# Staging buffers, splits and start blocks in a one-layer hybrid encoder: low weight blocks loaded into ystage, q and k split four blocks later, the first stick head two blocks later

## The chip, the cores and the metric

The kernel runs on one core of a Trainium2 chip. Its time is the device time of one execution in microseconds (us); the figure given for a kernel is the median of its runs. Five engines take part: PE (TensorE) multiplies, DVE (VectorE) and ACT (ScalarE) convert, scale and add, POOL (GpSimd) masks and issues the DMAs that add into their target, and SP (SyncE) issues the plain DMAs. Each engine takes its instructions in a fixed order, and a waiting instruction holds up all that stand behind it on its engine.

## The reference

One layer over 512 tokens of width 2048, all in float32:

```python
h = rms_norm(x, g0); P = h @ w_in                      # 11 blocks of 512 columns
y = concat(stick_breaking(q, k, v),                    # 8 heads of 64, causal
           differential(q, k, v, rel_bias),            # 4 heads, q and k 2 x 64
           rg_lru(...), short_conv(...))
x = x + rms_norm(y @ w_out, g1)
u = causal_dwconv(rms_norm(x, g2) @ w_up)              # 2048 x 8192
x = x + rms_norm((gelu(u[:, :4096]) * u[:, 4096:]) @ w_down, g3)
```

## The kernel before

Products are done in pairs of a rounded high part and a remainder ("hi" and "lo"), because PE multiplies in a rounded float32 form: an operand is cast by ACT (the hi part) and DVE subtracts to get the lo part. A weight chunk of 512 KB is loaded by SP into a `w_raw` tile, cast into `w_hi` and subtracted into `w_lo`; there are three buffers of each.

PE's order is written by hand. `group` (L127 to L180) walks eight chunks of a weight block over four output units; after every few matmuls it calls `tick()`, which advances a block counter, `clock[0]`, and runs the functions that `at(block, fn)` has put down for that block. A block of a plain group holds eight or four matmuls of 512 columns (8, 8, 4 and 4 in a chunk). So attention's small matmuls lie between the weight matmuls at fixed places, and the block numbers decide where.

The order of the other engines is not written by hand. A scheduler takes the program's instructions by a priority, which is their order in the program unless a `high_priority` block puts them ahead, and gives each engine what is ready in its own forecast of the run; what it has fixed is then each engine's order on the chip.

First half, groups 0 to 10 over `w_in`: 0 and 1 feed the recurrent branch, 2 is v of the stick heads, 3 and 4 their q and k, 5 is v of the differential heads, 6 and 7 their q and k, 8 to 10 the short convolution. `norm0` (L299) multiplies the sum of squares, `ssum`, by ones to get the first norm's factor; it stands at block 27, and group 0 ends with block 32. Lines 353 to 393 work out small parameters of the recurrent and the differential branch from the table `par`. `Scores.query` and `Scores.key` (L493, L504) evict a unit of q or k from PSUM by DVE, and return a function that splits it into hi and lo parts by ACT casts and DVE subtractions; `group` calls it right after the eviction. `stick` (L539) puts a head down from block t0: logits at t0 to t0+2, the sums at t0+7 to t0+9, weights at t0+9, values at t0+16; heads follow each other every 12 blocks, and the first starts two blocks after group 3 ends.

Second half: `w_out`, the residual and norm, then the FFN. Its first up columns are four plain groups: `up_plain(half, ts)` for both column halves over tokens 0 to 255 (H0), and then over tokens 256 to 511 (H1). All other up columns are 28 units (`up_unit`, numbers 4 to 31) of a Strassen-like scheme with seven products, `seven` (L1063): from the four blocks of a weight tile, a11, a12, a21 and a22, it forms s1 = a21 + a22, s2 = a11 + s1, s3 = a11 + a21 and s4 = a12 + s2, and multiplies in the order a11, a12, s2 ("T2"), s1 ("T1"), s3 ("T3"), s4 ("22"), a22 ("T4"). `raw` loads a block (SP), `dma_add` adds one into its target by a DMA from POOL (L1058), `add` adds by DVE (L1054), `operand` makes hi and lo (L1048, L1049), and `take` evicts a product (L1142 to L1145). Unit 4 is the first: its tiles a11, a12 and a21 are w_raw buffers, s3 and a22 are `spare[0]` and `spare[2]`, which lie in a "mg" buffer of the pool `wide` that is free only after `split_t2` has read it. The later units take a11 and a21 from `spare` and a12, s3 and a22 from w_raw.

The down part has four plain groups and then eight units (`down_unit`) through the same `seven`. Its operands are built by `build` (L1189 and on) from the gated values, which come in pairs through two staging pools, `ystage` and `gst`, of two buffers each; down unit 0 takes s3 from `ystage` and a22 from `gst`. In the up part nothing uses `ystage`.

Of the kernel before, what the change touches and what calls it, by code (L numbers as in the profile page):

```python
# [48 lines left out]
def trunk(ctx: ExitStack, tc: tile.TileContext, xT, params, consts, wgate, w_in, w_out, w_up0, w_up, w_dn, w_dns, out):  # L49
# [187 lines left out]
    with ExitStack() as ph:  # L237
# [83 lines left out]

        at(27, norm0)
        at(50, norm0_columns)
# [12 lines left out]
        def lru_group(pair, before=None):  # L336
            xs, gs = {}, {}

            def evac(u, ps):
# [5 lines left out]
                else:  # L345
# [7 lines left out]
        negb = ph1.tile([P, 8], F32, name="negb")  # L353
        V.tensor_scalar(out=negb, in0=par[:, PC["b_gate"]:PC["b_gate"] + 8], scalar1=-1.0, scalar2=0.0,
                        op0=ALU.mult, op1=ALU.add)
        lam_ap = par[:, PC["lam"]:PC["lam"] + 4]

        sp8 = ph1.tile([P, 4], F32, name="sp8")
# [4 lines left out]
        la_m = ph1.tile([P, 4], F32, name="la_m")  # L363
        V.scalar_tensor_tensor(out=la_e, in0=lam_ap, scalar=-1.0, in1=lam_ap, op0=ALU.mult, op1=ALU.max)
        A.activation(out=la_e, in_=la_e, func=AF.Exp, scale=-1.0)
        V.tensor_scalar(out=la_s, in0=la_e, scalar1=2.0, scalar2=0.0, op0=ALU.add, op1=ALU.add)
        V.reciprocal(out=la_s, in_=la_s)
        V.tensor_tensor(out=la_s, in0=la_s, in1=la_e, op=ALU.mult)
        V.tensor_tensor(out=la_q, in0=la_s, in1=la_s, op=ALU.mult)
        V.memset(la_m, 1.0 / 17)  # L370
        for n in (15, 13, 11, 9, 7, 5, 3, 1):
            V.tensor_tensor(out=la_m, in0=la_m, in1=la_q, op=ALU.mult)
            V.tensor_scalar(out=la_m, in0=la_m, scalar1=1.0 / n, scalar2=0.0, op0=ALU.add, op1=ALU.add)
        V.tensor_tensor(out=la_m, in0=la_m, in1=la_s, op=ALU.mult)
        V.tensor_scalar(out=la_e, in0=lam_ap, scalar1=-1.0, scalar2=0.0, op0=ALU.mult, op1=ALU.max)
        V.scalar_tensor_tensor(out=sp8, in0=la_m, scalar=2.0, in1=la_e, op0=ALU.mult, op1=ALU.add)
        V.tensor_scalar(out=sp8, in0=sp8, scalar1=8.0, scalar2=0.0, op0=ALU.mult, op1=ALU.add)
        V.tensor_scalar(out=nsp8, in0=sp8, scalar1=-1.0, scalar2=0.0, op0=ALU.mult, op1=ALU.add)

        lm = ph1.tile([P, 2], F32, name="lm")  # L380
        lmp = ph1.tile([P, 128], F32, name="lmp")
        dl = PC["dl"]
        for i in range(2):
            V.tensor_tensor(out=lmp[:, i * 64:(i + 1) * 64], in0=par[:, dl + 128 * i:dl + 128 * i + 64],
                            in1=par[:, dl + 128 * i + 64:dl + 128 * i + 128], op=ALU.mult)
            V.reduce_sum(out=lm[:, i:i + 1], in_=lmp[:, i * 64:(i + 1) * 64], axis=mybir.AxisListType.X)
        A.activation(out=lm, in_=lm, func=AF.Exp)
        lam = ph1.tile([P, 1], F32, name="lam")
        V.scalar_tensor_tensor(out=lam, in0=lm[:, 0:1], scalar=LAM_INIT, in1=lm[:, 1:2],
                               op0=ALU.add, op1=ALU.subtract)  # L390
        gsub = ph1.tile([P, 1], F32, name="gsub")
        V.tensor_scalar(out=gsub, in0=pc("sub_g"), scalar1=1.0 - LAM_INIT, scalar2=0.0,
                        op0=ALU.mult, op1=ALU.add)

# [92 lines left out]
        class Scores:  # L487
# [5 lines left out]
            def query(self, ps):  # L493
                f = t2()
                V.scalar_tensor_tensor(out=f, in0=ps, scalar=0.125, in1=rstd0, op0=ALU.mult, op1=ALU.mult)
                return lambda: self.split_query(f)

# [6 lines left out]
            def key(self, ps):  # L504
                f = t2()
                mul_rstd(f, ps)
                return lambda: self.split_key(f)

# [19 lines left out]
        def qk_group(g, dst):  # L528
            def evac(u, ps):
                return (dst[u // 2].query if u % 2 == 0 else dst[u // 2].key)(ps)  # L530
            in_group(g, evac)
# [6 lines left out]

        def stick(t0, pr, e, qk, vs):  # L539

# [101 lines left out]
        for g, prs in ((3, (0, 1)), (4, (2, 3))):  # L642
            qk = (Scores(), Scores())
            qk_group(g, qk)
            t0 = max(t0, clock[0] + 2)
            for i, pr in enumerate(prs):
                for e in range(2):
                    stick(t0, pr, e, qk[i], vs)
                    t0 += 12
# [134 lines left out]
    with ExitStack() as ph:  # L784
# [238 lines left out]
        ubs = up_ph.enter_context(tc.tile_pool(name="ubs", bufs=4))  # L1023
        for half in range(2):
            up_plain(half, H1)


        split_t2()
        ubp = ubs
        spare_t = wide.tile([P, 4, 4, S // 2], F32, name="mg")  # L1030
        spare = [spare_t[:, i] for i in range(4)]
        turn = [0]

# [6 lines left out]
        def raw(t, src):  # L1040
            with tc.high_priority(offset=AHEAD):
                w_load.append(nc.sync.dma_start(out=t, in_=by4(src)))
# [19 lines left out]

        def seven(src, tops, take, first=False, place=None):  # L1063

# [22 lines left out]
            if place is None:  # L1087
                a11, a21 = raw(spare[n], src[0, 0]), raw(spare[2 + n], src[1, 0])
                a12, s3, a22 = (w_raw() for _ in range(3))
            else:  # L1090
                a11, a12, a21 = (w_raw() for _ in range(3))
                s3, a22 = place
                raw(a11, src[0, 0])
                raw(a12, src[0, 1])
                raw(a21, src[1, 0])
            if first:
                raw(a22, src[1, 1])
                add(a21, a21, a22)
# [36 lines left out]
        def up_unit(unit):  # L1135
# [105 lines left out]
        def down_unit(n):  # L1241
            def take(i, ts, ps, first):
                u = 2 * n + i
                t = m3[u // 4][:, u % 4, ts]
                with tc.high_priority(offset=AHEAD):
                    for part in (ps[:, 0:256], ps[:, 256:512]):
                        V.tensor_tensor(out=t, in0=t, in1=part, op=ALU.subtract if i else ALU.add)  # L1247
# [173 lines left out]
```

## Time and profile before

| what | us |
|---|---|
| median of three runs (1768.4, 1771.96, 1774.53) | 1771.96 |
| the profiled execution | 1772.23 |
| its span, first to last instruction | 1770.5 |
| PE busy in the span | 1727.5 |
| DVE busy | 1252.2 |
| ACT busy | 902.1 |
| POOL busy | 162.0 |

The profiled execution lies 0.27 us over the median. 1.73 us of it lie outside the span. The page of the profile gives busy times, a chain of waits that ended last, and groups of instructions; the views of the trace give each engine's instructions in order of time with the idle time before them and what ended it, the waits in total, and busy time and granted clock by window.

### The profile page before, as it was taken

The page shows a single profiled execution, that of the slowest core. Times are in us where ns is not written, and L with a number is a line of the kernel's source. Part 1 is how long each engine was busy: PE and PEld are TensorE (multiplying, and loading weights), DVE is VectorE, ACT ScalarE, POOL GpSimd, SP SyncE. Part 2 cuts the span into 40 slices and gives each one's busy share as a digit, 9 for nine tenths or more (in the row PEclk, how much of TensorE's full clock was granted, in tenths as well). Part 3 has the DMA queues.
Part 4 walks back from the last instruction along what each step waited for, and adds up shares of the span by engine and source line. Part 5 has one row for each costly group of instructions (what it writes and reads, how often), then busy time and mean ns, then how long its engine had stood idle before and what let it go on. Part 6 is the DMA issues. An engine that isn't in the chain of part 4 may idle for free.

```text
span 1770.5 us, 24333 instructions
## 1 busy us (share of the span) xinstructions
PE 1727.5 (98%) x9152; PEld 1484.7 (84%) x9152; DVE 1252.2 (71%) x1926; ACT 902.1 (51%) x1351; POOL 162.0 (9%) x229
## 2 busy tenths in 40 slices
PE   8999999999999999999899999999999999999995
PEld 7778788887888888899888888888888888888884
DVE  7885565576656424799888888888878887775337
ACT  6443576665334235777555555555554673334342
POOL 0000011100000011100111111111111001100110
PEclk9999999999999999999999999999999999999998
DMA  7234222242223625775788898898888768878233
GB/s 258 80 102 144 74 79 87 78 154 73 93 86 101 208 96 173 236 225 184 220 237 252 231 231 217 229 239 230 223 238 225 211 203 229 215 198 280 96 116 134
DMA packets 97310, 309.14 MB, mean 175 GB/s; under 512 B 10500, under 2 KB 14852, under 8 KB 97192
## 3 DMA queue, kind: packets, MB, share of 16 engines
q1 hardware_dynamic: 80200, 247.81, 41.9%
q0 software_dynamic: 15840, 57.68, 17.5%
q10 hardware_dynamic: 1152, 2.10, 0.3%
q8 instruction: 72, 1.18, 0.3%
q14 instruction: 46, 0.38, 0.1%
HBM read 266.64 MB, written 21.24 MB: 163 GB/s over the span
## 4 chain that ended last, share of the span: by engine, by line
PE 89%; DVE 5%; DMA 3%; ACT 2%; issue 1%; POOLq 0%; POOL 0%; SPq 0%; DVEq 0%; ACTq 0%
PE mm L157 33%; PE mm L1079 24%; PE mm L1084 12%; PE pa L157 4%; PE pa L149 3%; PE mm L149 2%; PE mm L121 2%; PE mm L123 2%; PE mm L122 2%; PE pa L587 1%; DVE w_lo L100 1%; DMA w_raw<-in_w_up_dram 1%; DVE w_lo L1049 1%; PE pa L692 1%; DVE m L1298 0%
## 5 line engine op out<-in xcount | busy, mean ns | idle before, releaser
L100 DVE TENSOR_TENSOR w_lo<-w_raw,w_hi 128x1024 fp32r<-128x1024 f32 (+1 forms) x207 | 253.6, 1226 | 251.2 <-PE mm L157 141.1
L99 ACT CAST w_hi<-w_raw 128x1024 fp32r<-128x1024 f32 (+1 forms) x207 | 216.2, 1045 | 292.1 <-PE mm L157 195.1
L157 PE MATMUL mm<-a,w_hi 128*128 128x512 f32 (+1 forms) x1504 | 339.9, 377 | 2.1 <-DVE t L330 2.1
L157 PEld LDWEIGHTS mm<-a,w_hi 128*128 128x128 f32 x1504 | 267.1, 189 | 52.2 <-DVE t L330 2.6
L1079 PE MATMUL mm<-a,w_hi 128*128 128x512 f32 x1088 | 274.6, 395 | 6.8 <-DVE ub L1145 5.0
L1048 ACT CAST w_hi<-w_raw 128x1024 fp32r<-128x1024 f32 x146 | 153.1, 1050 | 201.7 <-PE mm L1079 169.0
L1079 PEld LDWEIGHTS mm<-a,w_hi 128*128 128x128 f32 x1088 | 197.0, 190 | 42.4 <-DVE ub L1145 5.4
L1049 DVE TENSOR_TENSOR w_lo<-w_raw,w_hi 128x1024 fp32r<-128x1024 f32 x146 | 178.4, 1222 | 39.0 <-ACT w_hi L1048 34.4
L157 PE MATMUL mm<-a,w_lo 128*128 128x512 f32 (+1 forms) x752 | 182.1, 380 | 0.0
L1084 PEld LDWEIGHTS mm<-a,w_lo 128*128 128x128 f32 x1088 | 148.9, 191 | 10.7
L157 PEld LDWEIGHTS mm<-a,w_lo 128*128 128x128 f32 x752 | 132.5, 190 | 24.0 <-issue 1.5
L1084 PE MATMUL mm<-a,w_lo 128*128 128x256 f32 x1088 | 152.1, 283 | 0.0
L1079 PE MATMUL mm<-xs,w_hi 128*128 128x512 f32 x576 | 144.5, 393 | 1.0 <-DVE ub L1145 1.0
L1048 ACT CAST w_hi<-mg 128x1024 fp32r<-128x1024 f32 x83 | 86.6, 1044 | 86.9 <-PE mm L1079 84.9
L1079 PEld LDWEIGHTS mm<-xs,w_hi 128*128 128x128 f32 x576 | 103.8, 189 | 19.9 <-DVE ub L1145 1.4
L1049 DVE TENSOR_TENSOR w_lo<-mg,w_hi 128x1024 fp32r<-128x1024 f32 x83 | 101.4, 1221 | 23.4 <-ACT w_hi L1048 23.4
L1079 PE MATMUL mm<-mg,w_hi 128*128 128x512 f32 x352 | 88.3, 393 | 1.5 <-DVE m L1247 1.5
L1084 PEld LDWEIGHTS mm<-xs,w_lo 128*128 128x128 f32 x576 | 78.6, 191 | 5.6
L1145 DVE TENSOR_TENSOR ub<-ub,mm 128x256 f32<-128x256 f32 x196 | 81.6, 416 | 0.0
L1084 PE MATMUL mm<-xs,w_lo 128*128 128x256 f32 x576 | 80.4, 283 | 0.0
L1079 PEld LDWEIGHTS mm<-mg,w_hi 128*128 128x128 f32 x352 | 63.4, 189 | 13.1 <-issue 1.9
L1247 DVE TENSOR_TENSOR m<-m,mm 128x256 f32<-128x256 f32 x112 | 46.7, 418 | 36.4 <-PE mm L1084 36.3
(306 smaller groups left out, 2656.9 us busy)
## 6 DMA issues: line engine op xcount, KB each, us to landing
w_raw<-in_w_up_dram SPq DMA_DIRECT2D x116, 512.0 KB, 5.3
w_raw<-in_w_in_dram SPq DMA_DIRECT2D x87, 512.0 KB, 3.4
mg<-in_w_up_dram SPq DMA_DIRECT2D x56, 512.0 KB, 4.6
w_raw<-in_w_out_dram SPq DMA_DIRECT2D x48, 512.0 KB, 3.5
w_raw<-in_w_dn_dram SPq DMA_DIRECT2D x38, 512.0 KB, 3.7
mg<-in_w_up_dram POOLq DMA_DIRECT2D x28, 512.0 KB, 7.8
w_raw<-in_w_up_dram POOLq DMA_DIRECT2D x27, 512.0 KB, 9.1
w_raw<-mg POOLq DMA_DIRECT2D x27, 512.0 KB, 6.0
```

The lines of the kernel that those rows point to most:

```text
L99: w_split.append(A.copy(out=hi[:, sl], in_=raw[:, sl]))
L100: V.tensor_tensor(out=lo[:, sl], in0=raw[:, sl], in1=hi[:, sl].bitcast(F32), op=ALU.subtract)
L121: T.matmul(ps, lhsT=sh, rhs=mh, start=first, stop=False)
L122: T.matmul(ps, lhsT=sh, rhs=ml, start=False, stop=False)
L149: T.matmul(pss[u][:, 0:256] if low else pss[u].rearrange("p (a t) -> p a t", a=2), lhsT=(wh, wl)[low][:, kk, us], rhs=both[k][:, 0, ts] if ...
L157: T.matmul(pss[u], lhsT=a, rhs=b, start=c == 0 and kk == 0 and not low and i == 0, stop=False)
L1048: w_split.append(A.copy(out=by4(hi), in_=v))
L1049: V.tensor_tensor(out=by4(lo), in0=v, in1=by4(hi).bitcast(F32), op=ALU.subtract)
L1079: T.matmul(ps.rearrange("p (a t) -> p a t", a=2), lhsT=hi[:, k * P:(k + 1) * P], rhs=tops[name][k], start=first and k == 0, stop=False, **kw)
L1084: T.matmul(ps[:, 0:256], lhsT=lo[:, k * P:(k + 1) * P], rhs=tops[name][k][:, 0], start=False, stop=k == 7, **kw)
L1145: taken.append(V.tensor_tensor(out=t, in0=t, in1=ps[:, 256:512], op=ALU.add))
L1247: V.tensor_tensor(out=t, in0=t, in1=part, op=ALU.subtract if i else ALU.add)
```

## The change

It has six parts.

1. `norm0` moves from block 27 to block 28.
2. The small parameters become a function that runs in the first block of group 1 and not right behind group 0.
3. `query` and `key` put their split down four blocks later with `at`, and return nothing.
4. `stick` takes `late`: for the first head (pair 0, e 0) all that follows its logits comes two blocks later.
5. Unit 4 of the up part: a21 and a22 (`low_row`) are loaded into `ystage`'s two buffers by instructions that stand ahead of `up_plain(1, H1)`; s3 stays in `spare[0]`; a11 and a12 stay in w_raw.
6. Down unit 0: a22 and s3 change places (a22 in `ystage`, s3 in `gst`).

```diff
-        at(27, norm0)
+        at(28, norm0)
...
-        V.tensor_scalar(out=negb, in0=par[:, PC["b_gate"]:PC["b_gate"] + 8], scalar1=-1.0, scalar2=0.0,
...
+        def small_parameters():
+            V.tensor_scalar(out=negb, in0=par[:, PC["b_gate"]:PC["b_gate"] + 8], scalar1=-1.0, scalar2=0.0,
...
+        at(clock[0] + 1, small_parameters)
...
             def query(self, ps):
...
-                return lambda: self.split_query(f)
+                at(clock[0] + 4, lambda: self.split_query(f))
...
             def key(self, ps):
...
-                return lambda: self.split_key(f)
+                at(clock[0] + 4, lambda: self.split_key(f))
...
-        def stick(t0, pr, e, qk, vs):
+        def stick(t0, pr, e, qk, vs, late):
...
             for n, bank in enumerate((1, 2, 0)):
                 at(t0 + n, lambda bank=bank: logits(bank))
+            t0 += late
             for n, bank in enumerate((2, 1, 0)):
                 at(t0 + 7 + n, lambda bank=bank: sums(bank))
...
-                    stick(t0, pr, e, qk[i], vs)
+                    stick(t0, pr, e, qk[i], vs, 2 if pr + e == 0 else 0)
...
-        for half in range(2):
-            up_plain(half, H1)
...
+        def stage(pool):
+            return by4(pool.tile([P, 2, S], F32, name="ys"))
+
+        up_plain(0, H1)
+
+        low_row = [raw(stage(ystage), w_up[0, 1, i]) for i in range(2)]
+        up_plain(1, H1)
...
             if place is None:
                 a11, a21 = raw(spare[n], src[0, 0]), raw(spare[2 + n], src[1, 0])
                 a12, s3, a22 = (w_raw() for _ in range(3))
+                dma_add(a21, by4(src[1, 1]))
             else:
-                a11, a12, a21 = (w_raw() for _ in range(3))
-                s3, a22 = place
-                raw(a11, src[0, 0])
-                raw(a12, src[0, 1])
-                raw(a21, src[1, 0])
-            if first:
-                raw(a22, src[1, 1])
+                a11, a12 = raw(w_raw(), src[0, 0]), raw(w_raw(), src[0, 1])
+                a21, a22, s3 = place()
                 add(a21, a21, a22)
-            else:
-                dma_add(a21, by4(src[1, 1]))
...
-            place = (spare[0], spare[2]) if unit == 4 else None
-            steps = seven(w_up[unit - 4], tops, take, unit == 4, place)
+            steps = seven(w_up[unit - 4], tops, take, (lambda: (*low_row, spare[0])) if unit == 4 else None)
...
-            place = [by4(t.tile([P, 2, S], F32, name="ys")) for t in (ystage, gst)] if n == 0 else None
-            for _ in seven(w_dns[n], dtops, take, n == 0, place):
+            def place():
+                return [raw(t, w_dns[0, 1, i]) for i, t in enumerate((w_raw(), stage(ystage)))] + [stage(gst)]
+
+            for _ in seven(w_dns[n], dtops, take, place if n == 0 else None):
```

More of the change, by code (lines that the diff above doesn't have):

```diff
@@ L353, in trunk @@
         negb = ph1.tile([P, 8], F32, name="negb")
-        V.tensor_scalar(out=negb, in0=par[:, PC["b_gate"]:PC["b_gate"] + 8], scalar1=-1.0, scalar2=0.0,
-                        op0=ALU.mult, op1=ALU.add)
-        lam_ap = par[:, PC["lam"]:PC["lam"] + 4]
         sp8 = ph1.tile([P, 4], F32, name="sp8")
@@ L363, in trunk @@
         la_m = ph1.tile([P, 4], F32, name="la_m")
[L364 to L377, printed above, removed]
@@ L378, in trunk @@
-        V.tensor_scalar(out=nsp8, in0=sp8, scalar1=-1.0, scalar2=0.0, op0=ALU.mult, op1=ALU.add)
         lm = ph1.tile([P, 2], F32, name="lm")
         lmp = ph1.tile([P, 128], F32, name="lmp")
+        lam = ph1.tile([P, 1], F32, name="lam")
+        gsub = ph1.tile([P, 1], F32, name="gsub")
+        lam_ap = par[:, PC["lam"]:PC["lam"] + 4]
         dl = PC["dl"]
[L383 to L393, printed above, removed]
+        def small_parameters():
+            V.tensor_scalar(out=negb, in0=par[:, PC["b_gate"]:PC["b_gate"] + 8], scalar1=-1.0, scalar2=0.0,
+                            op0=ALU.mult, op1=ALU.add)
+            V.scalar_tensor_tensor(out=la_e, in0=lam_ap, scalar=-1.0, in1=lam_ap, op0=ALU.mult, op1=ALU.max)
+            A.activation(out=la_e, in_=la_e, func=AF.Exp, scale=-1.0)
+            V.tensor_scalar(out=la_s, in0=la_e, scalar1=2.0, scalar2=0.0, op0=ALU.add, op1=ALU.add)
+            V.reciprocal(out=la_s, in_=la_s)
+            V.tensor_tensor(out=la_s, in0=la_s, in1=la_e, op=ALU.mult)
+            V.tensor_tensor(out=la_q, in0=la_s, in1=la_s, op=ALU.mult)
+            V.memset(la_m, 1.0 / 17)
+            for n in (15, 13, 11, 9, 7, 5, 3, 1):
+                V.tensor_tensor(out=la_m, in0=la_m, in1=la_q, op=ALU.mult)
+                V.tensor_scalar(out=la_m, in0=la_m, scalar1=1.0 / n, scalar2=0.0, op0=ALU.add, op1=ALU.add)
+            V.tensor_tensor(out=la_m, in0=la_m, in1=la_s, op=ALU.mult)
+            V.tensor_scalar(out=la_e, in0=lam_ap, scalar1=-1.0, scalar2=0.0, op0=ALU.mult, op1=ALU.max)
+            V.scalar_tensor_tensor(out=sp8, in0=la_m, scalar=2.0, in1=la_e, op0=ALU.mult, op1=ALU.add)
+            V.tensor_scalar(out=sp8, in0=sp8, scalar1=8.0, scalar2=0.0, op0=ALU.mult, op1=ALU.add)
+            V.tensor_scalar(out=nsp8, in0=sp8, scalar1=-1.0, scalar2=0.0, op0=ALU.mult, op1=ALU.add)
+            for i in range(2):
+                V.tensor_tensor(out=lmp[:, i * 64:(i + 1) * 64], in0=par[:, dl + 128 * i:dl + 128 * i + 64],
+                                in1=par[:, dl + 128 * i + 64:dl + 128 * i + 128], op=ALU.mult)
+                V.reduce_sum(out=lm[:, i:i + 1], in_=lmp[:, i * 64:(i + 1) * 64], axis=mybir.AxisListType.X)
+            A.activation(out=lm, in_=lm, func=AF.Exp)
+            V.scalar_tensor_tensor(out=lam, in0=lm[:, 0:1], scalar=LAM_INIT, in1=lm[:, 1:2],
+                                   op0=ALU.add, op1=ALU.subtract)
+            V.tensor_scalar(out=gsub, in0=pc("sub_g"), scalar1=1.0 - LAM_INIT, scalar2=0.0,
+                            op0=ALU.mult, op1=ALU.add)
@@ L529, in evac @@
             def evac(u, ps):
-                return (dst[u // 2].query if u % 2 == 0 else dst[u // 2].key)(ps)
+                (dst[u // 2].query if u % 2 == 0 else dst[u // 2].key)(ps)
             in_group(g, evac)
@@ L1023, in trunk @@
         ubs = up_ph.enter_context(tc.tile_pool(name="ubs", bufs=4))
-        for half in range(2):
-            up_plain(half, H1)
[L1028 to L1032, printed above, removed]
         def flat(t):
@@ L1043, in raw @@
             return t
+        def stage(pool):
[3 more added lines that the diff above has]
+        up_plain(1, H1)
+        split_t2()
+        ubp = ubs
+        spare_t = wide.tile([P, 4, 4, S // 2], F32, name="mg")
+        spare = [spare_t[:, i] for i in range(4)]
+        turn = [0]
         def operand(v):
@@ L1061, in w_raw, with seven @@
             return by4(wp.tile([P, 2, S], F32, name="w_raw"))
-        def seven(src, tops, take, first=False, place=None):
+        def seven(src, tops, take, place=None):
             lo_, hi_ = slice(0, 256), slice(256, 512)
@@ L1119, in seven @@
             take(0, hi_, x, True)
-            if not first:
+            if place is None:
                 raw(a22, src[1, 1])
```

## The prediction

> **What bounds the kernel now.** I read the page first, then the waits of PE in total, then PE in order of time for each wait, and last the granted clock around each.
>
> ```profile
> span 1770.5 us, 24333 instructions
> PE 89%; DVE 5%; DMA 3%; ACT 2%; issue 1%; POOLq 0%; POOL 0%; SPq 0%; DVEq 0%; ACTq 0%
> ```
>
> PE carries 89% of the chain that ended last. With PE's work unchanged, only its waits, and the slow matmuls that follow a wait, can be won. The rows below are PE's, in order of time, with the idle time before each and what ended it.
>
> ```profile
> 46.28 1.12 PE L301 MATMUL pa<-vd,con 128*128 128x512 f32 x2 [1.22 <-DVE vd L279]
> 209.29 0.85 PE L587 MATMUL pa<-t,tri_r 128*128 128x256 f32 x2 [1.62 <-ACT t L571]
> 425.38 1.33 PE L157 MATMUL mm<-a,w_hi 128*128 128x512 f32 x4 [2.15 <-DVE t L330]
> 858.25 2.00 PE L1079 MATMUL mm<-a,w_hi 128*128 128x512 f32 x8
> 865.86 3.78 PE L1079 MATMUL mm<-a,w_hi 128*128 128x512 f32 x8 [4.66 <-DVE ub L1145]
> 894.02 2.11 PE L1079 MATMUL mm<-xs,w_hi 128*128 128x512 f32 x8 [0.86 <-DVE ub L1145]
> 908.68 2.12 PE L1079 MATMUL mm<-a,w_hi 128*128 128x512 f32 x8 [0.37 <-DVE ub L1145]
> 1463.04 2.06 PE L1079 MATMUL mm<-a,w_hi 128*128 128x512 f32 x8 [1.74 <-DVE m L1247]
> ```
>
> Seven waits lie where the change touches: 1.22 + 1.62 + 2.15 + 4.66 + 0.86 + 0.37 + 1.74 = 12.6 us. Three drag a slow clock behind them (windows; the columns are busy time by engine, then PEclk):
>
> ```profile
> 211.20:214.65 3.45, 3.45 (x12) 2.87 (x11) 1.11 (x4) 1.98 (x3) 0.79 (x2) 0.51 0.08 31
> 426.20:429.70 3.50, 3.50 (x13) 3.02 (x12) 1.65 (x4) 3.27 (x5) 0.00 (x0) 0.51 0.10 41
> 863.20:870.00 6.80, 4.14 (x11) 3.37 (x12) 4.49 (x6) 2.81 (x5) 0.28 (x1) 0.50 1.01 210
> ```
>
> At half the clock, half of PE's busy time is lost: 1.7, 1.7 and 2.1 us. So at most 12.6 + 5.5 = 18.1 us can be won. After the wait of 1.74 at 1463.04 eight matmuls took 2.06, the full pace.
>
> A rule speaks against counting the clock in full. The Trainium skill, "TensorE: Matmul & The Clock Gate", Part 1, says that the clock halves after an idle window of about 3.4 us; by it only the wait of 4.66 would cost clock, and the sum below would be 3.4 us smaller at most. The trace disagrees: 1.62 and 2.15 were enough, so that sum gets no chance of its own.
>
> **norm0 and the small parameters.** PE comes to `norm0` four matmuls later. Sixteen take 3.63 us here:
>
> ```profile
> 224.61 3.63 PE mm L157 x16
> L372 DVE TENSOR_TENSOR la_m<-la_m,la_q 128x4 f32<-128x4 f32 x6 | 0.9, 157 | 0.0
> L279 DVE TENSOR_TENSOR vd<-vd,t 128x512 f32<-128x512 f32 x12 | 8.3, 692 | 0.1
> ```
>
> Four are 0.91 us. The sum of squares still ends when it did, so 1.22 - 0.91 = 0.31 of the wait stays: **-0.9** (bounds 0 and -1.2). The evictions of group 0 get their factor at the same time, since the matmul was bound by `ssum`.
>
> The small parameters' DVE rows (second and third row: DVE groups from 36 to 46.3 us) already run among the squares, before group 0 ends, though they stand behind it in the program. DVE runs what is ready. Between the old place and the new one lie only loads, casts and matmuls of group 1, so their order stays: **0** (bounds 0 and -0.9, if those six of 0.157 left the squares' chain).
>
> **The first stick head.** Sums, weights and values come two blocks later, 8 + 4 matmuls, 2.7 us. The sums of bank 2 waited 1.62 for the last lo part:
>
> ```profile
> 208.57 1.13 DVE L572 TENSOR_TENSOR t<-t,t 128x512 fp32r<-128x512 f32 x2
> 212.27 0.69 DVE L572 TENSOR_TENSOR t<-t,t 128x512 fp32r<-128x512 f32 x1 [0.72 <-ACT t L571]
> ```
>
> It ends at 208.57 + 1.13 = 209.7; PE now arrives at 207.7 + 2.7 = 210.4. Bank 0's lo part ends at 212.96, and its sums come near 214. Both are covered, so wait and slow clock go: 1.62 + 1.7 = **-3.3** (bounds 0 and -3.3). The next head's logits stay at t0+12 and now share ACT with this head's weights, three casts; its sums are seven blocks behind, about 10 us.
>
> **The splits.** The wait of 2.15 is for the last key's eviction, on DVE in this order:
>
> ```profile
> 422.54 1.23 DVE L100 TENSOR_TENSOR w_lo<-w_raw,w_hi 128x1024 fp32r<-128x1024 f32 x1 [0.83 <-ACT w_hi L99]
> ...
> 423.93 0.69 DVE L502 TENSOR_TENSOR big<-t,big 64x512 fp32r<-64x512 f32 x1
> 424.63 0.69 DVE L330 TENSOR_TENSOR t<-mm,rstd 128x512 f32<-128x512 f32 x1
> ```
>
> A query's split (L502) stood ahead of the eviction (L330), and a weight's lo part ahead of both. Four blocks later the split still is ready when it was; it only gives way where something else is ready too. If the eviction goes first, wait and clock are gone: -3.9. If the order stays: 0. The nearest row is the L502 itself: without it alone the wait is 1.4 and the clock may hold. I take about half, **-2.0**. The 8 casts and 4 subtractions of each pair of heads move together; what may be late next is the first head of groups 3 and 6, two blocks behind the group's end:
>
> ```profile
> 369.74 0.61 ACT L516 CAST big<-big 64x512 fp32r<-64x512 f32 x1
> ...
> 373.35 0.22 PE L525 MATMUL pa<-big 128*128 128x128 f32 x1
> ```
>
> The first key's last cast ended at 370.35, 3.0 us before PE wanted it. That is the cover.
>
> **The first up unit.** s2 needs a11 and s1, and s1 needs a21, which was the last to get a buffer and to land (the first row is of the chain of waits):
>
> ```profile
> 852.03 6.85 DMA w_raw<-in_w_up_dram
> 853.23 1.24 DVE L1049 TENSOR_TENSOR w_lo<-w_raw,w_hi 128x1024 fp32r<-128x1024 f32 x1
> 858.98 1.23 DVE L1054 TENSOR_TENSOR w_raw<-w_raw,mg 128x1024 f32<-128x1024 f32 x1 [1.39 <-DMA w_raw<-in_w_up_dram]
> 860.78 1.22 DVE L1054 TENSOR_TENSOR w_raw<-w_raw 128x1024 f32<-128x1024 f32 x1
> 860.90 0.63 ACT L983 ACTIVATE f<-f 128x512 f32<-128x512 f32 x1 [3.22 <-DVE f L980]
> 862.03 1.99 ACT L1048 CAST w_hi<-w_raw 128x1024 fp32r<-128x1024 f32 x2 [0.51 <-DVE w_raw L1054]
> 863.93 0.37 ACT L1142 COPY ub<-mm 128x256 f32<-128x256 f32 x1
> 865.39 0.41 DVE L1145 TENSOR_TENSOR ub<-ub,mm 128x256 f32<-128x256 f32 x1
> ```
>
> It lands at 858.88; s1 and s2 end at 862.0; the casts of s2 and s1 hold ACT until 864.0, and the copy that empties the first product (finished near 858.3) stands behind them. PE waits for that.
>
> With a21 and a22 in `ystage`, s1 is long done. s2 follows a11's lo part at 853.23 + 1.24 = 854.5 and ends at 855.7; its cast ends near 857, its lo part near 859; the copy finds ACT free at about 858.5 (it sat idle for 3.22 us before 860.90), and DVE's half follows by 860. PE is due at 858.25 + 2.8 = 861. So the wait and its clock go, 4.66 + 2.1 = 6.8; I leave 0.3 for a lo part ahead of DVE's half. s3's load keeps its buffer, and its adding DMA on POOL goes no later than before. The product of s4 was started once s2 stood, so that DMA goes some 5 us sooner. One w_raw load and one mg load of 512 KB leave SP's queue at 852, one w_raw buffer is free for unit 5, and `spare[2]` for unit 6. So the waits of 0.86 and 0.37 should go too, but PE comes 6.5 us earlier to transfers that the DMA engines must carry by then; I take half, 0.6. Sum **-7.1** (bounds 0 and -8.0).
>
> The two loads do not vanish. Priority and free memory decide when they go: at once when the first half's memory is free.
>
> ```profile
> L777 SPq DMA_DIRECT2D t<-y_d x12: 319/327/1199, 359.4 to 584.5; - x12
> L840 SPq DMA_DIRECT2D xs<-in_xT_dram x8: 384/468/572, 589.3 to 601.5; - x8
> 587.00:606.00 19.00, 19.00 (x86) 15.74 (x85) 6.44 (x15) 5.26 (x6) 0.00 (x0) 1.00 0.85 298
> ```
>
> The second half's first loads go at 589.3. I expect the new ones beside them: 1 MB at 298 GB/s, an estimate of 3.5 us more of a crowded stretch. PE was busy 19.00 of 19.00 us in it, and three weight buffers of 24 matmuls (5.4 us) each are the cover: 0. Without it a late chunk costs its 3.5 us. The addition, 1.23 us, waits on DVE for these loads; behind it stand the lo parts of `w_out` chunks, with the same cover.
>
> By the Trainium skill, "DMA: Bandwidth & Descriptors", section "Issuing engines are not separate DMA queues", DMAs of SP and POOL interleave on the same 16 engines, which speaks against a free load; its price would be the 3.5 us above.
>
> **Down unit 0.** a22 now takes the staging buffer that is free first (first row: two issues within 3.3 us, the second at their end):
>
> ```profile
> 1446.51 3.30 SPq L1042 DMA_DIRECT2D ys<-in_w_dns_dram x2
> 1453.46 1.22 DVE L1054 TENSOR_TENSOR w_raw<-w_raw,ys 128x1024 f32<-128x1024 f32 x1 [0.22 <-DMA ys<-in_w_dns_dram]
> 1462.48 0.94 DVE L1247 TENSOR_TENSOR m<-m,mm 128x256 f32<-128x256 f32 x2
> ```
>
> s1 waited for a22's landing and can start some 3 us sooner. But DVE is nearly full there, and PE waits for L1247 at the end of its queue. Half of 1.74, **-0.9** (bounds 0 and -1.7). s3 lands 3 us later and is wanted two products behind.
>
> **Sum:** 0.9 + 3.3 + 2.0 + 7.1 + 0.9 = 14.2; 1772.2 - 14.2 = **1758.0**. The base is the profiled execution, which stands 0.3 over the median; I leave that.
>
> **The rivals.**
> - *The wait is handed on* (0.18). Units 5 and 6 come to blocks that have not landed, so that only 2 of the 7.1 stay: 1763. For it: two waits already there. Against: units 5 and 6 get two buffers earlier.
> - *It does not do what it says* (0.09). DVE's order of evictions and splits stays, and s1's addition is put late in DVE's order, so that unit 4 waits as before: 14.2 - 2.0 - 7.1 = 5.1 is left, less the down part's 0.9: 1768.
> - *The first key is late* (0.07). Its six casts are put behind what stands in the four blocks; past 3.0 us PE waits. At 6 us late, 3.0 and a slow clock of 1.7, in groups 3 and 6: 1758 + 2 x 4.7 = 1767.4.
> - *Buffers taken early*, the slower side (0.06). s1 and a22 are ready from about 600 us, so their casts could take two of three `w_hi` and `w_lo` buffers until unit 4. Then each of the 72 chunks cast from 600 to 846 waits at least its cast of 1.05: 1772 + 75 = 1847. The point is whether buffers go to who is ready or by program order. The y loads (L777) speak for the latter: the first y tiles were stored from 95.8 us, and yet their first load is at 359.4, when the last stick head had its tiles.
>
> ```profile
> L334 SPq DMA_DIRECT2D y_d<-t x12: 320/327/331, 95.8 to 581.7; - x12
> L99 ACT CAST w_hi<-w_raw 128x1024 fp32r<-128x1024 f32 x72 | 75.3, 1048 | 73.1 <-PE mm L157 42.6 <-PE mm L149 15.1 <-PE pa L149 7.1
> ```
>
> **How the numbers follow.** Forecast 0.60. All bounds at once give 1772 - 18.1 = 1754; the three runs lie up to 3.6 under their median, so I go to 1752. Upwards the range takes in the second and third rivals, to 1768.5. About 0.3% (5.3 us) is what a measurement of this kernel can tell from no change. Forecast and handed-on wait lie under 1766.7: faster 0.78. The second and third rivals lie within it: same 0.16. Slower 0.06.
>
> **What would show it.** Right: no PE wait over 1 us near 208, 421 and 858, no half clock there, the two ys loads near 590, s2's L1054 some 5 us sooner before the unit's second product ends, T2 at full pace. Wrong: a wait for L1054 or L1145 in units 5 or 6, a wait of L520 or L525 for a cast of L516, or `w_hi` casts with waits of a microsecond in every chunk of the `w_out` groups.

## The result, and the profile after

The changed kernel takes 1762.22 us (median of six runs, 1760.3 to 1764.59); the kernel before took 1771.4 beside it (six runs, 1768.4 to 1774.53). The ratio is 0.995, with a 95% interval of 0.9938 to 0.9963: 9 us faster, against 14.2 forecast (1758.0). The profiled execution took 1762.23, and its span is 1760.5 where it was 1770.5.

The page of the changed kernel, its span and the shares of the chain that ended last:

```profile
span 1760.5 us, 24333 instructions
...
PE 88%; DVE 5%; ACT 3%; DMA 2%; issue 1%; SPq 0%; POOL 0%; POOLq 0%; DVEq 0%; ACTq 0%
```

PE still carries the chain, so the waits of PE are again what to read. In order of time (start, length, engine, line, operation; in brackets the idle time before it and what ended it):

```profile
46.77 1.13 PE L301 MATMUL pa<-vd,con 128*128 128x512 f32 x2 [0.32 <-DVE vd L279]
210.79 0.84 PE L591 MATMUL pa<-t,tri_r 128*128 128x256 f32 x2 [0.56 <-ACT t L575]
852.17 2.00 PE L1090 MATMUL mm<-a,w_hi 128*128 128x512 f32 x8
857.33 2.11 PE L1090 MATMUL mm<-a,w_hi 128*128 128x512 f32 x8 [2.20 <-DVE ub L1150]
865.67 2.58 PE L1090 MATMUL mm<-xs,w_hi 128*128 128x512 f32 x8 [2.49 <-DVE ub L1150]
1454.27 2.08 PE L1090 MATMUL mm<-a,w_hi 128*128 128x512 f32 x8 [0.68 <-DVE m L1251]
```

The wait at the q and k eviction near 421 has no row any more. In units 5 and 6 the waits of 0.86 and 0.37 are gone too. But unit 4 has two waits, 2.20 and 2.49, where it had one of 4.66, and there is still a half clock behind the second. Both kernels do the same 9152 matmuls, and apart from the few that parts 1 and 4 move they do them in the same order, so the start of one matmul in both traces tells how much has been won up to it. The product on a12 started at 858.25 and now starts at 852.17: 6.1 us were won up to there. Done for more places (a matmul of the same number in each trace, times of the kernel before):

| stretch, us | part | forecast | seen |
|---|---|---|---|
| 30 to 206 | norm0, small parameters | -0.9 | -0.6 |
| 206 to 290 | first stick head | -3.3 | -2.2 |
| 290 to 432 | q and k splits | -2.0 | -4.0 |
| 760 to 1000 | unit 4 and the units behind it | -7.1 | -1.6 |
| 1450 to 1470 | down unit 0 | -0.9 | -1.0 |

The rest is a start 0.5 later, 0.3 lost near 732, 0.6 won near 1610 and 0.6 at the tail; in all -10.0, the difference of the spans. The first three rows gave 6.8 where 6.2 were forecast, and that nearness is luck: the splits gave 2.0 more than forecast and the stick head 1.1 less. The miss is unit 4.

**What stands in unit 4.** ACT in order of time, changed kernel, and then the rows of DVE that end the two waits:

```profile
852.28 0.38 ACT L1012 COPY ub<-pa 128x256 f32<-128x256 f32 x1
853.45 1.29 ACT L988 ACTIVATE f<-f 128x512 f32<-128x512 f32 x2 [0.80 <-DVE f L985]
854.65 1.03 ACT L1059 CAST w_hi<-ys 128x1024 fp32r<-128x1024 f32 x1
855.59 0.36 ACT L1147 COPY ub<-mm 128x256 f32<-128x256 f32 x1
858.05 1.05 ACT L1059 CAST w_hi<-mg 128x1024 fp32r<-128x1024 f32 x1 [2.10 <-DMA mg<-in_w_up_dram]
862.98 1.04 ACT L1059 CAST w_hi<-w_raw 128x1024 fp32r<-128x1024 f32 x1 [3.88 <-DMA w_raw<-w_raw]
863.93 0.37 ACT L1147 COPY ub<-mm 128x256 f32<-128x256 f32 x1
```

```profile
855.72 1.22 DVE L1060 TENSOR_TENSOR w_lo<-ys,w_hi 128x1024 fp32r<-128x1024 f32 x1 [0.46 <-ACT w_hi L1059]
856.86 0.41 DVE L1150 TENSOR_TENSOR ub<-ub,mm 128x256 f32<-128x256 f32 x1
864.05 1.23 DVE L1060 TENSOR_TENSOR w_lo<-w_raw,w_hi 128x1024 fp32r<-128x1024 f32 x1 [3.36 <-ACT w_hi L1059]
865.20 0.41 DVE L1150 TENSOR_TENSOR ub<-ub,mm 128x256 f32<-128x256 f32 x1
```

L1147 is the copy with which `take` begins to empty a product, and L1150 is DVE's half, which ends it. The first product was done when the second began, at 852.17, but its copy ran at 855.59: ahead of it stood two Gelus of plain units (L988), which waited for their convolutions on DVE, and a cast. DVE's half came later still, at 856.86, behind the lo part (L1060) that goes with that same cast. That is the wait of 2.20. T2 was done when T1 began, at 860.2; its copy ran at 863.93, behind the cast of s4 at 862.98, with DVE's half again behind the lo part, and that cast waited for the adding DMA that makes s4:

```profile
850.41 0.88 POOL L1069 DMA_DIRECT2D mg<-in_w_up_dram  x1 [77.77 <-DVE w_raw L1065]
853.25 0.87 POOL L1069 DMA_DIRECT2D w_raw<-in_w_up_dram  x1 [1.96 <-DMA mg<-in_w_up_dram]
853.99 1.02 POOL L1069 DMA_DIRECT2D w_raw<-w_raw  x1
```

```profile
w_raw<-w_raw POOLq DMA_DIRECT2D x1, 512.0 KB, 8.9
```

(POOL in order of time; then the view of DMA issues for the last of the three: size in KB, us from issue to landing.) It landed at 862.9. That is the wait of 2.49. In the kernel before it had gone out at 862.61 (POOL):

```profile
862.61 0.86 POOL L1058 DMA_DIRECT2D w_raw<-w_raw  x1 [0.22 <-issue]
```

### The profile page after: what moved, and what is told of

The parts are those of the page before. It is cut to its first block, busy times and chain, and to the rows that moved or that the text cites. A ratio compares the mean times of both kernels' runs of the same rounds, so it can differ in the third digit from the quotient of the medians.

```text
span 1760.5 us, 24333 instructions
## 1 busy us (share of the span) xinstructions
PE 1724.1 (98%) x9152; PEld 1480.6 (84%) x9152; DVE 1252.6 (71%) x1926; ACT 901.8 (51%) x1351; POOL 164.8 (9%) x229
## 4 chain that ended last, share of the span: by engine, by line
PE 88%; DVE 5%; ACT 3%; DMA 2%; issue 1%; SPq 0%; POOL 0%; POOLq 0%; DVEq 0%; ACTq 0%
PE mm L157 30%; PE mm L1090 25%; PE mm L1095 13%; PE pa L157 3%; PE pa L149 3%; PE mm L149 2%; PE mm L121 2%; PE mm L123 2%; PE mm L122 2%; DVE w_lo L100 1%; PE pa L591 1%; ACT w_hi L99 1%; DVE vd L279 1%; PE pa L697 1%; DMA w_raw<-w_raw 1%
## 5 line engine op out<-in xcount | busy, mean ns | idle before, releaser
L100 DVE TENSOR_TENSOR w_lo<-w_raw,w_hi 128x1024 fp32r<-128x1024 f32 (+1 forms) x207 | 253.4, 1225 | 242.4 <-PE mm L157 130.2
L1060 DVE TENSOR_TENSOR w_lo<-w_raw,w_hi 128x1024 fp32r<-128x1024 f32 x145 | 177.1, 1222 | 37.3 <-ACT w_hi L1059 36.9
L1060 DVE TENSOR_TENSOR w_lo<-mg,w_hi 128x1024 fp32r<-128x1024 f32 x82 | 100.1, 1221 | 22.5 <-ACT w_hi L1059 22.5
L1150 DVE TENSOR_TENSOR ub<-ub,mm 128x256 f32<-128x256 f32 x196 | 81.5, 416 | 0.0
```

The source lines that it names most:

```text
L100: V.tensor_tensor(out=lo[:, sl], in0=raw[:, sl], in1=hi[:, sl].bitcast(F32), op=ALU.subtract)
L1060: V.tensor_tensor(out=by4(lo), in0=v, in1=by4(hi).bitcast(F32), op=ALU.subtract)
L1150: taken.append(V.tensor_tensor(out=t, in0=t, in1=ps[:, 256:512], op=ALU.add))
```

## The experiments

All kernels compute the whole layer. Each ratio is against runs of the kernel before on the same chip. Parts alone first, then unit 4.

| kernel | median, us | ratio to before (95%) |
|---|---|---|
| before + parts 1 and 4 (late_only) | 1766.53 | 0.9981 (0.9972 to 0.999) |
| before + parts 2 and 3 (splits_small) | 1770.54 | 1.0007 (0.9998 to 1.0015) |
| before + parts 1 to 4 (late_splits) | 1765.09 | 0.9975 (0.9965 to 0.9986) |
| before + part 5 (up_only) | 1768.8 | 0.9989 (0.998 to 0.9999) |
| after, s4's DMA first on POOL (s4_first) | 1760.98 | 0.9943 (0.9927 to 0.9959) |
| after, s4's cast behind T2's copy (cast_behind) | 1761.04 | 0.9942 (0.9928 to 0.9957) |
| after, all gates later (gates_later) | 1769.99 | 0.9991 (0.9981 to 1.0002) |
| after, gates later, cast behind (gates_cast) | 1767.68 | 0.998 (0.9971 to 0.9989) |
| after, gates later, cast behind, s4 first (gates_pool_cast) | 1764.86 | 0.9976 (0.9965 to 0.9987) |
| after, two gates later, cast behind (half_gates_cast) | 1765.88 | 0.9976 (0.9967 to 0.9984) |
| after, two gates later, s4 on DVE (half_gates_dve) | 1761.46 | 0.9952 (0.9938 to 0.9966) |
| after, s4 on DVE (s4_dve) | 1760.18 | 0.9947 (0.9932 to 0.9962) |

### The first stick head alone

```diff
-        at(27, norm0)
+        at(28, norm0)
...
+            t0 += late
```

> The kernel before with two edits only: norm0's first statistics one block later and the first stick head's sums two blocks later. Theory A (the trace of the changed kernel: this part gave 0.6 to 0.9 before 206 us and 2.6 at 208, of which 0.45 came back at 273): about 1770.7 - 3.0 = 1767.7, a wait of 0.5 to 0.6 left at the first sums. Rival (the prediction's size: 0.9 + 3.3 with the wait and its slow clock gone whole; the rest of 0.56 seen there comes from the splits, which changed the order of casts on ACT): the wait at the first sums is gone, about 1766.5.

1766.53, 3.3 below the 1769.81 of the kernel before beside it; the interval takes in both forecasts, so the waits have to tell. No wait is left at the first sums, and PE won 3.8 between 206 and 225 us. So the rival, which is the prediction's size, holds for the stick head. The wait at `norm0` fell from 1.22 to 0.31, and PE won 0.6 there.

### The splits alone

```diff
-                return lambda: self.split_query(f)
+                at(clock[0] + 4, lambda: self.split_query(f))
...
-                return lambda: self.split_key(f)
+                at(clock[0] + 4, lambda: self.split_key(f))
```

> The kernel before with the splits of q and k put four blocks behind their evictions and with the small parameters taken out of the start; nothing else. Theory A (the trace of the changed kernel: PE gained 4.0 between 290 and 432 us, that is the wait of 2.15 near 420 and all the slow clock behind it): about 1770.7 - 4.0 = 1766.7, no wait over 0.3 near 421 and no half clock at 426. Rival (the prediction's -2.0: half the wait stays, or part of the 4.0 belongs to the first stick head, whose casts stand near these): about 1768.7.

Theory A holds near 421: PE won 4.0 there, with the wait and the half clock gone. Yet the time is that of the kernel before. PE at the first stick head's sums, in this kernel:

```profile
211.85 0.95 PE L591 MATMUL pa<-t,tri_r 128*128 128x256 f32 x2 [3.27 <-ACT t L575]
```

The wait was 1.62. On ACT the casts of the delayed splits now stand among that head's functions until 207.2 (the last had ended at 204.6), and the cast of bank 2 that the sums need ran at 211.39 (it was 208.84). So 1.6 went there and 0.6 near 279. By the traces 1.8 should be left; the median shows none of it, with -0.4 the best end of its interval (ratio 0.9998). What took the rest isn't settled. The trace of the kernel before, with which all traces are compared here, is of an execution of 1772.23, 2.4 over the median of the runs beside this experiment (1769.81); part of that may be the clock, of which more at the end.

### Both together, without the feed-forward part

```diff
 (parts 1 to 4 of the change; the up units and the down units as before)
```

> The kernel before with norm0, the small parameters, the first stick head and the q and k splits as in the changed kernel, and nothing changed in the feed-forward part. Theory A (the splits alone made the first sums wait 3.3 in place of 1.6, since their casts moved ahead of that stick head's own on ACT; the two blocks of lateness cover that, so the two parts are worth more together than apart): -6.1 by 760 us as in the changed kernel, then the old wait of unit 4 and its half clock: 1769.8 - 6 = about 1764. Rival (the parts add as measured apart, -3.3 and +0.7): about 1767.

1765.09, nearer to theory A. PE won 6.2 between 185 and 432 us, and the first sums waited for

```profile
209.97 0.85 PE L591 MATMUL pa<-t,tri_r 128*128 128x256 f32 x2 [0.56 <-ACT t L575]
```

the same 0.56 as in the changed kernel. Two blocks of lateness cover most of what the splits put ahead of those casts. The intervals of the medians alone would not tell -4.7 from the -2.6 that the two parts give apart; the waits do.

### The up unit alone

```diff
+        low_row = [raw(stage(ystage), w_up[0, 1, i]) for i in range(2)]
         up_plain(1, H1)
...
+            steps = seven(w_up[unit - 4], tops, take, (lambda: (*low_row, spare[0])) if unit == 4 else None)
```

> The kernel before with the first up unit's lower row loaded ahead into the staging buffers, and nothing else changed (down unit 0 keeps its buffers). Theory A (the two waits of the changed kernel, 2.20 at T2 and 2.49 with a half clock at T3, are of the order that the edit itself leaves on ACT and POOL): they come here too, 6 us later, and the time falls by 1.6 only: about 1769. Rival (they come because PE, DVE and ACT reach unit 4 six us sooner, against transfers that did not move; the edit alone keeps its 7.1): no wait over 1 us in unit 4, about 1763.6.

1768.8, and PE in unit 4:

```profile
862.79 2.12 PE L1085 MATMUL mm<-a,w_hi 128*128 128x512 f32 x8 [1.99 <-DVE ub L1145]
871.02 2.91 PE L1085 MATMUL mm<-xs,w_hi 128*128 128x512 f32 x8 [2.38 <-DVE ub L1145]
```

The same two waits, 5 us later. Theory A holds: the order that the edit leaves on ACT and POOL makes them, and not that PE came earlier. By the ratios this part and late_splits add to 6.4 us, where the whole change gave 8.9; the intervals, some 2 us to each side, take in the difference.

### One swap on POOL

```diff
-            dma_add(s3, by4(src[1, 0]))
+            with tc.issue_after(s4_adds[0].ins) if len(s4_adds) == 1 else nullcontext(): dma_add(s3, by4(src[1, 0]))
```

> The changed kernel with one swap on POOL's queue: unit 4's s4 addition (adding DMA) is issued ahead of unit 5's s3 addition. Theory A (ACT's queue: the copy that empties T2 stands behind s4's cast, and that cast waits for s4's DMA, issued 853.99 and landed 862.88 behind unit 5's DMA): the DMA goes near 851.5 and lands near 860.4, the wait of 2.49 at T3 falls under 0.5 and the 3.41 us at half clock after it go, so 1762.2 - 2.0 - 1.7 = about 1758.5. Rival B (the DMA is slow because the 16 DMA engines are crowded there, so its place in POOL's queue counts for little): it lands after 862, the wait stays over 1.5, time within 1 us of 1762.2. Rival C (handed on: what unit 4 gains, units 5 and 6 lose to blocks that land late): the wait goes, new waits of 2 to 4 us in units 5 or 6, time within 1.5 us of 1762.2.

The wait at T3 is gone, as A says. But the DMA was issued at 853.12 and took 8.8 to land, at 861.9, so B was right about its speed; and this time the wait of T2 had a half clock behind it:

```profile
858.66 3.48 PE L1090 MATMUL mm<-a,w_hi 128*128 128x512 f32 x8 [2.52 <-DVE ub L1150]
```

Eight matmuls took 3.48, where the changed kernel's took 2.11 behind the same wait. PE won 2.6 in unit 4 over the changed kernel (a matmul at 853 lay 1.0 behind it, one at 872 lay 1.6 ahead). Units 5 and 6 have no new wait, so C is out; but the time, 1760.98, is not the 1758.5 of A.

### One swap on ACT

```diff
-            o4 = operand(s4)
+            with tc.issue_after(copies[1].ins) if len(copies) == 3 else nullcontext(): o4 = operand(s4)
```

> The changed kernel with one swap on ACT's queue: the cast of s4 stands behind the copy that empties T2 instead of ahead of it; the DMA that makes s4 stays where it is (issued 853.99). Theory A: T2 ended near 860.3, so the copy runs near 860.5 instead of 863.93, the wait of 2.49 at T3 goes whole, with the half clock after it (1.7): about 1758.0, and s4's late landing (862.88) costs nothing, since its product is the last but one of the unit. Rival B (the late DMA itself is what PE waits for): a wait of about 2 us comes at the product of s4 instead, time within 1 us of 1762.2. Rival C (handed on to units 5 and 6): the wait goes, new ones of 2 to 4 us there, time within 1.5 us of 1762.2.

```profile
857.11 2.11 PE L1090 MATMUL mm<-a,w_hi 128*128 128x512 f32 x8 [2.31 <-DVE ub L1150]
...
866.81 2.11 PE L1090 MATMUL mm<-a,w_hi 128*128 128x512 f32 x8 [1.05 <-DVE ub L1150]
```

The wait at T3 went, with its clock; the DMA landed at 862.9 as before. So the copy had waited in ACT's line, and not for its own data. A smaller wait of 1.05 came at the product of s4: part of rival B. PE won 2.9 in unit 4. Of that and of the 2.6 above the medians show about 1, within their intervals. In the traces 0.6 of this one and 1.3 of the one above went again in the down units, where waits of the same code differ from kernel to kernel, and 1.3 of each went at the tail, where each has a half-clock window (from 1739.70 and from 1742.28) that the changed kernel lacks.

### The gates out of unit 4

```diff
-                    gates[u] = conv(ub[half, u], half, u)
+                    pass
...
-                    later.append(lambda: glu(u, gates[u], conv(ub[half, u], half, u)))
+                    later.append(lambda: glu(u, conv(ub[0, u], 0, u), conv(ub[half, u], half, u)))
```

> The changed kernel with the gate convolutions and Gelus of the plain up units (0 to 3) taken out of unit 4's start and made in units 4 to 7 beside the value convolutions. Theory A (T2's wait of 2.20 at 857.33 comes from ACT's queue: copy of the first product at 855.59 behind two Gelus that wait for DVE's convolutions): the copy runs near 853, the wait falls under 0.5, and the time falls by 1.5 to 2.2, to about 1760; the wait at T3 stays. Rival B (the wait is that of s2's or s1's own blocks, which land or are cast late): the wait stays over 1.5, time within 1 us of 1762.2. Rival C (the moved work, 2.9 us on DVE and ACT for each of four units, makes units 4 to 7 wait): time 1763 or more.

T2's wait went whole: 2.5 were won by 858. Then PE waited 7.65 at T3, where it had waited 2.49. POOL, in this kernel, with the view of DMA issues for the first row of them:

```profile
849.38 1.83 POOL L1069 DMA_DIRECT2D mg<-in_w_up_dram  x2 [77.45 <-DMA mg<-in_w_up_dram]
851.87 0.86 POOL L1069 DMA_DIRECT2D w_raw<-in_w_up_dram  x1 [0.66 <-DMA mg<-in_w_up_dram]
857.75 0.89 POOL L1069 DMA_DIRECT2D w_raw<-w_raw  x1 [5.02 <-issue]
```

```profile
mg<-in_w_up_dram POOLq DMA_DIRECT2D x1, 512.0 KB, 8.1
```

With DVE emptier, one more addition got ahead: that of unit 4's own s3 went first, two of later units next, and s4's came fourth. It stood ready and was held for 5 us; "issue" means that the profile names nothing that it waited for. It went 0.31 after the first one landed, at 857.44, 8.1 us after its issue at 849.38. PE paid for it:

```profile
867.68 3.78 PE L1090 MATMUL mm<-xs,w_hi 128*128 128x512 f32 x8 [7.65 <-DVE ub L1150]
```

The time, 1769.99, lies where rival C put it (1763 or more), but not by its way alone: against the changed kernel the trace lost 3.7 in unit 4, by this wait, which none of the three theories had, 1.4 in unit 8 and 2.5 in the down units. The wait gave theory D, of three adding DMAs under way at most. The same with s4's cast behind the copy:

```diff
 (the two edits above together)
```

> Both edits: gate convolutions of the plain units made in units 4 to 7, and the cast of s4 behind the copy that empties T2. Theory A (both new waits of unit 4 come from what stands ahead on ACT's queue): 2.2 and 4.2 us go, 1762.2 - 6.4 = about 1756, near the term of -7.1 that was forecast for unit 4 and 1.6 of which was seen. Rival C (handed on to units 5 and 6, whose blocks must come that much sooner): the waits go and come again there, time 1760 to 1762.

1767.68: neither. Waits of 0.5 at T3 and 5.2 at the product of s4, which is held up the same way (issued at 857.68, landed at 864.83).

### The limit on POOL

```diff
 (gates later, s4's cast behind T2's copy, s4's adding DMA ahead of unit 5's s3)
```

> The changed kernel with three edits: the gate convolutions of the plain units made in units 4 to 7, the cast of s4 behind the copy that empties T2, and s4's adding DMA ahead of unit 5's s3 addition on POOL. Theory D (POOL has at most three adding DMAs under way: with the gates moved, units 5 and 6 got their s1 additions in at 849.4 and 850.3 and unit 5 its s3 at 851.9, s4 came fourth and was issued at 857.75, 0.31 after the first of them landed at 857.44; so the wait of T3 grew to 7.8): as third in the queue, s4 goes near 852, lands near 861 to 862, its cast no longer holds the copy, and unit 4's waits sum to under 1.5, in place of 7.8 with gates moved alone: unit 4 gains some 5 us over the changed kernel; what later units lost by the moved gates (1.4 near 950) stays: 1757 to 1759. Rival E (the fourth DMA was late for another reason, the place of its operands in DVE's order or crowded DMA engines): s4 goes after 856 or lands after 864, and a wait of 4 us or more stays in unit 4: 1765 or more.

```profile
848.42 0.88 POOL L1069 DMA_DIRECT2D mg<-in_w_up_dram  x1 [76.67 <-DVE w_lo L1060]
849.56 0.87 POOL L1069 DMA_DIRECT2D mg<-in_w_up_dram  x1 [0.26 <-issue]
850.33 0.99 POOL L1069 DMA_DIRECT2D w_raw<-w_raw  x1
856.77 0.88 POOL L1069 DMA_DIRECT2D w_raw<-in_w_up_dram  x1 [5.45 <-issue]
```

Theory D holds: as third, s4's DMA went at 850.33, and now it is the other one, as fourth, that was held until 0.32 after the first landing, at 856.45. The forecast of the time did not hold: among three adding DMAs s4's took 11.1 to land, PE waited 2.73 for its product, and units 6 and 8 waited 1.20 and 1.25 more.

### Two gates only

```diff
-                    gates[u] = conv(ub[half, u], half, u)
+                    if u < 2: gates[u] = conv(ub[half, u], half, u)
```

With it `later` makes the gates of units 2 and 3, and s4's cast stands behind the copy.

> The changed kernel with two edits on ACT's queue, POOL's queue unchanged: the gate convolutions of plain units 2 and 3 (the two whose Gelus stood ahead of the first copy) are made in units 6 and 7, and the cast of s4 stands behind the copy that empties T2. Theory F (the copies of unit 4 stood in line first behind the Gelus, then behind s4's cast; with both out of the way the landing of s4's own DMA, 862.9, is the next bound: its cast and lo part end near 865.2, and the copy that empties T1 stands behind that cast): T2's wait of 2.20 goes, and a wait of 2.5 to 3.5 comes at the product of s4 (it was 1.05 with the cast moved alone), so nothing is gained over that run: 1760 to 1762. Rival G (s4's DMA, now issued earlier with PE's pace, lands in time): no wait over 1 us in unit 4, 1757.

```profile
855.86 2.11 PE L1090 MATMUL mm<-a,w_hi 128*128 128x512 f32 x8 [0.17 <-DVE ub L1150]
867.36 2.11 PE L1090 MATMUL mm<-a,w_hi 128*128 128x512 f32 x8 [2.69 <-DVE ub L1150]
947.62 3.19 PE L1090 MATMUL mm<-a,w_hi 128*128 128x512 f32 x8 [1.78 <-DVE ub L1150]
```

Theory F holds in unit 4, with 0.17 at T2 and 2.69 at s4's product. The time, 1765.88, does not: in the trace, unit 8 waited 1.78, with a half clock behind it, and lost 3.3 to the changed kernel. All five kernels with moved gates have a wait of 1.2 to 1.8 there, and no other has one.

### s4 without a DMA

```diff
-            dma_add(a12, s2)
+            add(a12, a12, s2) if dve and dve.pop() else dma_add(a12, s2)
```

First with the two gates moved, then alone.

> The changed kernel with the gate convolutions of plain units 2 and 3 made in units 6 and 7, and unit 4's s4 added on DVE (1.23 us, both operands are in SBUF) instead of by an adding DMA of POOL (8.9 us from issue to landing). Theory F: s4 stands by 854, nothing late is left ahead of unit 4's copies, its waits sum to under 1 us, no half clock there: 2.20 + 2.49 + 1.7 = 6.4 under the changed kernel's 1762.2, about 1756. Rival C (handed on): units 5 and 6, reached 6 us sooner, wait for blocks that have not landed: 1759 to 1761, with new waits of 2 to 5 us there. Rival H (DVE is the next bound: its 1.23 for s4 delays lo parts): waits for w_lo in unit 4, 1759 or more.

> The changed kernel with only unit 4's s4 addition moved from POOL's adding DMA to DVE. Theory F: the wait at T3 (2.49) and its half clock (1.7) go; T2's wait shrinks by about half, since one of the two Gelus ahead of the first copy now stands behind it and the other still waits for DVE: about 1757.5. Rival C (handed on to units 5 and 6): 1760 to 1762.

PE in the first of the two, and in the second:

```profile
862.06 2.11 PE L1090 MATMUL mm<-xs,w_hi 128*128 128x512 f32 x8 [1.21 <-DVE ub L1150]
945.11 3.31 PE L1090 MATMUL mm<-a,w_hi 128*128 128x512 f32 x8 [1.78 <-DVE ub L1150]
```

```profile
855.69 2.11 PE L1090 MATMUL mm<-a,w_hi 128*128 128x512 f32 x8 [2.21 <-DVE ub L1150]
```

In the first, unit 4 won 4.9 over the changed kernel, of the 6.4 expected. The 1.21 that stayed is DVE's half of T2's `take` behind the lo part of s4, as rival H had it in kind. 3.4 went again at 945, where DVE works off the moved gates; units 5 and 6 have no new wait, against C. In the second the wait at T3 and its clock went, 4.3 us; T2's stayed at 2.21, not half. PE came there 1.65 sooner, and DVE's half of the `take`, behind the lo part as in the changed kernel, again began about 1.7 after PE was due. Its median, 1760.18, is the smallest of all, but its interval lies over that of the changed kernel. So no version here is shown to beat it; what is shown is how unit 4's waits come and go.

## Why the prediction was right and wrong

- **norm0 and small parameters** (-0.9 and 0): the wait fell by 0.90, from 1.22 to 0.32, as worked out from four matmuls. PE kept 0.6 of it; 0.3 went again by 54 us.
- **The first stick head** (-3.3): right for this part alone (3.8 in late_only). With the splits it gave 2.2: 0.56 of the wait stayed, and 0.5 came back by 290. I had costed the two parts one by one, but both put work in the same line on ACT, and the splits alone took there what they gave at 421.
- **The splits** (-2.0): the mechanism was right, and the size was too small. The eviction (L330) does go ahead. DVE, changed kernel:

```profile
418.88 0.69 DVE L519 TENSOR_TENSOR big<-t,big 64x512 fp32r<-64x512 f32 x1
419.60 0.69 DVE L330 TENSOR_TENSOR t<-mm,rstd 128x512 f32<-128x512 f32 x1
420.20 0.28 DVE L679 TENSOR_SCALAR t<-t,mx 128x128 f32<-128x128 f32 x1
420.40 1.22 DVE L100 TENSOR_TENSOR w_lo<-w_raw,w_hi 128x1024 fp32r<-128x1024 f32 x1
```

  The lo part (L100), which stood ahead of it, now stands behind it; a key's split (L519) still runs before it, but it ends at 420.29, before PE comes to the matmul that waited, near 420.7. Halving between 0 and -3.9 was a choice, and in this pair of traces the full value came. 1.7 of it is clock, which the same wait did not cost in late_only (below), and alone the splits gained nothing that a median shows. The first key was not late.
- **The up unit** (-7.1, seen -1.6): this is the step that failed, and in it the sentence "the copy finds ACT free at about 858.5 (it sat idle for 3.22 us before 860.90)". That idle time belonged to an instruction, the Gelu that waited for DVE's convolutions, and the copy can stand behind it. Then s4's DMA did go earlier, by 8.6 and not 5, but its cast was put ahead of T2's copy. By the sign that the prediction itself had named (no wait over 1 us near 858, and no half clock) this part was wrong. Summed: 4.66 + 0.86 + 0.37 of waits and 2.1 of clock went, 8.0; 2.20 + 2.49 of waits and 1.7 of clock came, 6.4; 1.6 is left. The rest of the step held: the loads from `ystage` went early and were hidden, s2 was added at 849.08, and the waits of units 5 and 6 went.
- **The rivals.** As I put it, the handed-on wait did not come: units 5 and 6 lost their waits and did not lack weights. A wait was handed on inside unit 4, in the order of ACT's line. That 1762.2 came, near the 1763 of this rival, is luck, since that price stood on waits in units 5 and 6.
- **Down unit 0** (-0.9): the wait fell from 1.74 to 0.68. But in four kernels that keep the old down unit its longest wait was 0 (splits_small), 0.47, 0.72 and 1.35, so neither the size nor that the change did it is shown.
- **The clock.** I counted the half clock as part of each wait. It is not (below).

## What to carry to other kernels

Idle time of an engine that works in order is not room: ask which instruction stands there waiting, and whether the one you move will stand behind it. A copy that empties a product is little work, but PE stands behind it, so it goes ahead of casts whose operands come by DMA (one such swap won 2.9 us of unit 4 in its trace, though no median shows a gain). And parts of a change that share an engine's line have to be summed together, since one can pay for the other.

## What was not expected of the hardware

**Adding DMAs of POOL: three under way.** In all fourteen traces never more than three of POOL's adding DMAs of 512 KB were between issue and landing. Where a fourth was ready it was issued 0.31 or 0.32 us after the first of them landed (in ten traces). While they run, the DMA engines are full at about half the rate. Windows of the changed kernel (length, then busy us of PE, weight loads, DVE, ACT and POOL with their instructions, PE's granted clock, share of the DMA engines, GB/s):

```profile
853.46:856.87 3.41, 1.67 (x12) 1.34 (x10) 2.95 (x8) 2.46 (x4) 1.54 (x2) 1.00 1.01 228
856.87:860.29 3.42, 2.96 (x17) 2.62 (x18) 1.98 (x5) 1.05 (x1) 0.88 (x1) 1.00 1.07 211
863.70:867.11 3.41, 1.44 (x6) 1.22 (x7) 3.02 (x4) 1.81 (x4) 0.00 (x0) 1.00 1.04 222
867.11:870.53 3.42, 3.42 (x13) 3.03 (x13) 0.54 (x2) 1.04 (x1) 0.00 (x0) 0.50 1.01 406
```

The first three hold adding DMAs and move 211 to 228 GB/s; the last, where they end, 406.

**The half clock goes by a fixed raster.** The same wait cost clock in one run and none in another: 2.15 at 425 in the kernel before, with a half clock; 2.15 at the same eviction in late_only, without. The windows of both:

```profile
422.86:426.28 3.42, 1.27 (x6) 0.77 (x5) 3.31 (x8) 3.04 (x8) 0.00 (x0) 1.00 0.43 120
426.28:429.69 3.41, 3.41 (x13) 2.93 (x12) 1.55 (x4) 3.17 (x5) 0.00 (x0) 0.50 0.08 34
```

```profile
417.74:421.15 3.41, 1.73 (x8) 1.11 (x6) 2.53 (x7) 3.36 (x8) 0.00 (x0) 1.00 0.08 12
421.15:424.57 3.42, 2.95 (x17) 2.58 (x18) 2.31 (x6) 3.01 (x5) 0.00 (x0) 1.00 0.35 141
```

In one trace the half clocks start whole multiples of 3.413 us apart (before: 211.23, 426.28 and 863.18, 63 and 128 of them apart). I cut the thirteen traces that have one before the tail into windows on that raster, from 100 to 1730 us. Where PE, at full clock, idled more than 1.8 of the 3.41 us of a window, the next one was at half clock, each time; where it idled under 1.5, none was; between, both occur. In the rows above 1.97 (the third) had a half clock behind it and 1.74 (the first) had none. So a wait of 2 us costs 1.7 more when it falls into one window, and nothing when two share it so that neither idles 1.5. Such a chance of 1.7 at each of several waits may be part of what runs of one kernel differ by: over the 72 runs of the kernel before beside the experiments, time and granted clock go together with a correlation of -0.41. The Trainium skill, "TensorE: Matmul & The Clock Gate", Part 1, says that the window is 4096 cycles, 3413 ns, and free-running; the traces agree to the digit. They differ from its word "idle window": a window about half idle was enough.

**Left open.** The waits of the down units differ between kernels with the same code there, by up to 1.7 us near 1454 (1.74 in the kernel before, none in splits_small) and by up to 1.2 near 1600 (0.79 and 2.02), and take back part of what unit 4 wins. What sets them was not tried.
